# Block products for queries and keys in a trunk layer: seven for eight over two pairs and two token blocks

## The chip, the cores and the metric

The kernel runs on one core of a Trainium2 chip. The core has a matrix engine (PE, with its weight loads shown apart as PEld), a vector engine (DVE), a scalar engine (ACT), a general engine (POOL), and a queue engine (SP) that here issues almost all transfers between DRAM and the core's SBUF. Each engine takes its instructions strictly in order and waits for semaphores of others. The metric is the device time of one execution in microseconds, lower is better. The profile is one execution, taken by the hardware profiler.

## The reference, cut to what matters

One layer, sequence 2048, model width 1024, float32:

```python
h = rms_norm(x, g_attn[l]) * (1.0 + scale_a) + shift_a
proj = h @ w_in[l]
q_f, k_f, v_f, q_s, k_s, v_s, f_logit = jnp.split(proj, offsets, axis=-1)
o_fox = forgetting_attention(split_heads(q_f, N_HEADS_FOX), split_heads(k_f, N_HEADS_FOX), ...)
o_sb = stick_breaking_attention(split_heads(q_s, N_HEADS_SB), split_heads(k_s, N_HEADS_SB), ...)
x = x + gate_a * (mix @ w_out[l])
h = rms_norm(x, g_mlp[l]) * (1.0 + scale_m) + shift_m
u = causal_depthwise_conv(h @ w_up[l], conv_w[l], conv_b[l])
x = x + gate_m * ((jax.nn.silu(u_gate) * u_val) @ w_down[l])
```

Each kind of attention (stick-breaking, "sb", and forgetting, "fox") has 8 heads of 64, taken as 4 pairs of 128 columns. Both are causal.

## The kernel before

**Stages.** First h = the normalized and modulated x, made for four blocks of 512 tokens (TB) and stored to DRAM as `hs`. Then attention, in 32 units, first sb and then fox: `units` lists kind, pair p and block tb, written here (sb, p, tb). Then the output projection, the gated MLP and the last norm, which the change leaves alone; they begin at about 1462 us in the profile.

**A product in three matmuls.** Every float32 operand is kept as two parts (`split`: ACT rounds the high part, POOL or DVE subtracts it for the low part), and a product is three matmuls: high x high, high x low, low x high. `accumulate` (L340 to L342) does that for queries and keys: eight slices of the inner dimension, three matmuls of 512 columns each, 24 for a query or key block of one pair.

**Projection as a filler.** `proj` (L462) makes queries, keys and, for even p, the values of two pairs, of one unit: it loads the eight h tiles of the block (L468, tile `hp`, ten buffers, 512 KB each), accumulates the queries, then the keys (`finish_proj`, L342), and for even p the values (L413, 256 columns each). Results go to DRAM (`qk_...`, L380 and L394; `vs_...`, L440), and `load_unit` reads them back as Q, K, V (L362 to L364). Weights are loaded once a pair (`load_w`, L314 to L321, tile `raw_qk` or `raw_v`, three buffers) and stay split in SBUF.

**Attention.** For a unit, `logits` (L596, L597) makes the logits of 128 queries against up to 512 keys. In sb (`sb_head`) ACT takes two sigmoids (L630, L631), POOL masks the diagonal (L633), and DVE runs a scan along the keys (L636). `weighted` transposes (L606), copies on ACT (L610), subtracts on DVE (L611), and multiplies with V (L615). `head_var` squares on POOL (L711), and the output goes to DRAM (L740, `os`). fox has a reduction on DVE (L675) and an exponential on ACT (L679).

**What sets the order.** `project` is a generator that goes through the units in order, one `yield` for every few matmuls; `pace` says how many of its steps are due after each step of the attention, so that a unit is projected by 80% of the unit ahead of it, and otherwise evenly from unit 3 to unit 30. `interleave` mixes them with fillers of their own pace (`late_mod` from unit 12 on). A scheduler then orders the instructions of each engine, so that program order alone does not tell where an instruction stands; the order is fixed when the program is built.

## Time and profile before

| | |
|---|---|
| runs | 2942.75, 2951.94 and 2953.25 us, median 2951.94 |
| profiled execution | span 2941.4 us from the first to the last instruction; it is not known which of the runs it resembles, and the lowest run lies 1.35 us above this span |
| DMA over the span | 601.89 MB, mean 205 GB/s |
| granted PE clock | 0.993 of full speed |
| queries and keys, all blocks (L342) | 1512 matmuls of 512 columns into `ps_pj` |
| values (L413) | 1536 matmuls |

An engine's busy time is the union of its instructions; a matmul's own duration contains its way through the array, so the cost of one in a row is best read from windows in which PE does nothing else. Windows give, for a stretch of time, each engine's busy us with the number of instructions in brackets, then the granted clock, the DMA engines' busy share and GB/s. A group's row is: line, engine, operation, out<-in, shapes, xcount | busy us, mean ns of one | idle time before them and what ended it.

### The profile page before, as it was taken

To read this page: it belongs to the slowest core of one execution; us is meant where nothing else is said; L and a number is where in the kernel's file an instruction comes from. 1 tells how busy PE (TensorE), PEld (TensorE's weight loads), DVE (VectorE), ACT (ScalarE), POOL (GpSimd) and SP (SyncE) were. 2 spreads that over 40 slices of the span, in tenths; PEclk is the share of its full clock that TensorE was granted. 3 is DMA by queue.
4 is the path that set the end of the run, shared out by engine and by line. 5 is a ranking of instruction groups with operands and counts; after the bars stand their busy time and mean duration, and the time that the engine had idled before them with its cause. 6 is when DMAs were issued, how large, how long until landed. Compare 5 with 4: busy or idle time off the path is not lost.

```text
span 2941.4 us, 45922 instructions
## 1 busy us (share of the span) xinstructions
PE 2867.8 (97%) x15772; PEld 2459.7 (84%) x15772; DVE 2179.5 (74%) x3464; ACT 1686.0 (57%) x3187; POOL 901.1 (31%) x967
## 2 busy tenths in 40 slices
PE   8999999999999999999999999999999999999998
PEld 7888888888988988888888788888788888888887
DVE  5787778877886656658843788888998888575476
ACT  5776767677776656658744554444444445433342
POOL 0431322243032423231213344444254543142200
PEclk8999999999999999999999999999999999999999
DMA  9749756867469794794537775554754444975644
GB/s 293 255 139 321 236 188 207 301 211 229 162 212 356 269 277 139 232 323 140 182 120 233 245 232 128 130 136 129 236 132 125 130 130 132 309 257 185 216 158 151
DMA packets 348346, 601.89 MB, mean 205 GB/s; under 512 B 34672, under 2 KB 178800, under 8 KB 348112
## 3 DMA queue, kind: packets, MB, share of 16 engines
q1 hardware_dynamic: 324208, 558.06, 57.7%
q0 software_dynamic: 10880, 20.97, 4.3%
q10 hardware_dynamic: 13024, 19.93, 1.9%
q8 instruction: 124, 2.03, 0.3%
q14 instruction: 110, 0.90, 0.1%
HBM read 420.77 MB, written 177.02 MB: 203 GB/s over the span
## 4 chain that ended last, share of the span: by engine, by line
PE 46%; DMA 3%; DVE 2%; SPq 1%; ACT 1%; issue 1%; POOL 0%; DVEq 0%; ACTq 0%; POOLq 0%
PE ps_o L1315 19%; PE ps_t L1315 7%; PE ps_o L1614 6%; PE ps_t L1614 3%; PE ps_bc L1614 3%; PE ps_o L912 1%; PE ps_pv L615 1%; DMA r<-rstd 1%; PE ps_bc L912 1%; PE ps_pt L606 1%; PE ps_o L1609 1%; DMA wo<-wos 1%; DMA hm<-hf_m 1%; SPq L895 1%; DVE op L46 1%
## 5 line engine op out<-in xcount | busy, mean ns | idle before, releaser
L1315 PE MATMUL ps_o<-op,wu 128*128 128x512 f32 x2592 | 608.0, 389 | 2.0 <-DVE snap L1366 1.5
L1315 PEld LDWEIGHTS ps_o<-op,wu 128*128 128x128 f32 x2592 | 486.2, 188 | 103.9 <-DVE snap L1366 1.9
L611 DVE TENSOR_TENSOR at<-ps_pt,at 128x512 fp32r<-128x512 f32 (+1 forms) x576 | 366.1, 652 | 100.2 <-ACT at L610 97.3
L636 DVE TENSOR_TENSOR_SCAN a<-r,a 128x512 f32<-128x512 f32 (+2 forms) x320 | 368.3, 1167 | 77.8 <-ACT a L631 39.9
L342 PE MATMUL ps_pj<-hp,w_qk 128*128 128x512 f32 x1512 | 411.2, 403 | 14.5 <-DMA hp<-hs 12.9
L610 ACT ACTIVATE at<-ps_pt 128x512 fp32r<-128x512 f32 (+1 forms) x576 | 318.5, 576 | 139.1 <-PE ps_pt L606 123.1
L615 PE MATMUL ps_pv<-at,V 128*128 128x256 f32 x2216 | 386.8, 292 | 9.3 <-DVE at L611 4.2
L615 PEld LDWEIGHTS ps_pv<-at,V 128*128 128x128 f32 x2216 | 320.9, 190 | 39.8 <-DVE at L611 11.4
L342 PEld LDWEIGHTS ps_pj<-hp,w_qk 128*128 128x128 f32 x1512 | 275.4, 190 | 71.0 <-DMA hp<-hs 16.2
L45 ACT ACTIVATE wu<-wuraw 128x512 fp32r<-128x512 f32 x204 | 128.9, 632 | 248.5 <-PE ps_o L1315 190.1
L596 PE MATMUL ps_qk<-K,Q 128*128 128x512 f32 (+2 forms) x640 | 265.7, 416 | 5.6 <-ACT a L631 3.3
L413 PE MATMUL ps_pj<-w_v,hp 128*128 128x256 f32 (+1 forms) x1536 | 236.6, 288 | 2.1 <-DVE hp L422 1.6
L597 PE MATMUL ps_qk<-K,Q 128*128 128x512 f32 (+2 forms) x640 | 235.7, 369 | 0.0
L1315 PE MATMUL ps_t<-op,wu 128*128 128x512 f32 x888 | 220.8, 390 | 1.0 <-DVE op L46 1.0
L413 PEld LDWEIGHTS ps_pj<-w_v,hp 128*128 128x128 f32 x1536 | 209.0, 189 | 10.9 <-DVE q L373 1.5
L630 ACT ACTIVATE r<-ps_qk 128x512 f32<-128x512 f32 (+2 forms) x320 | 173.1, 541 | 58.2 <-PE ps_qk L597 55.5
L46 DVE TENSOR_TENSOR wu<-wuraw,wu 128x512 fp32r<-128x512 f32 x204 | 189.6, 930 | 18.1 <-ACT wu L45 16.7
L1315 PEld LDWEIGHTS ps_t<-op,wu 128*128 128x128 f32 x888 | 166.4, 188 | 36.5 <-DVE op L46 1.8
L606 PE MATMUL ps_pt<-edge,a 128*128 128x128 f32 x1088 | 185.1, 274 | 8.4 <-DVE a L636 7.8
L1614 PE MATMUL ps_o<-op 128*128 128x512 f32 x840 | 191.5, 389 | 0.0
L1614 PEld LDWEIGHTS ps_o<-op 128*128 128x128 f32 x840 | 157.7, 188 | 32.7
L679 ACT ACTIVATE p<-p,mn 128x128 f32<-128x128 f32 (+15 forms) x128 | 153.9, 1203 | 53.3 <-DVE mn L675 52.2
(342 smaller groups left out, 5237.6 us busy)
## 6 DMA issues: line engine op xcount, KB each, us to landing
hp<-hs SPq DMA_DIRECT2D x224, 512.0 KB
wuraw<-in_w_up_dram SPq DMA_DIRECT2D x80, 512.0 KB
ra<-g SPq DMA_DIRECT2D x136, 256.0 KB
rb<-in_w_down_dram SPq DMA_DIRECT2D x108, 256.0 KB
g<-u SPq DMA_DIRECT2D x80, 256.0 KB
hs<-hp SPq DMA_DIRECT2D x32, 512.0 KB
hp<-in_w_ada_dram SPq DMA_DIRECT2D x32, 512.0 KB
qk_fox<-q SPq DMA_DIRECT2D x32, 512.0 KB
```

The source lines that it names most:

```text
L46: (lo_engine or nc.gpsimd).tensor_sub(lo, src, f(hi))
L342: nc.tensor.matmul(acc, w[kt][:, a, n], h[:, bb], start=kt == 0 and i == 0, stop=kt == KT - 1 and i == 2)
L413: nc.tensor.matmul(av[:, t * width:(t + 1) * width], hts[kt][:, a, tok], w[1][kt][:, bb, 0:width], start=kt == 0 and m == 0, stop=kt == KT ...
L596: nc.tensor.matmul(b[:, :cw], Q[:, hl, 0, qcols], K[:, hl, :cw], start=True, stop=False)
L597: marks.append(nc.tensor.matmul(b[:, :cw], Q[:, hl, 1, qcols], K[:, hl, :cw], start=False, stop=True).ins)
L606: nc.tensor.transpose(b[:, i * P:(i + 1) * P], blk(kts[kk], qi), ident)
L610: copies = [nc.scalar.activation(at[:, 0, lo:], b[:, lo:], AF.Copy).ins, nc.vector.tensor_sub(at[:, 1, lo:], b[:, lo:], f(at[:, 0, lo:])).ins]
L611: nc.vector.tensor_sub(at[:, 1, lo:], b[:, lo:], f(at[:, 0, lo:])).ins]
L615: m = nc.tensor.matmul(o[:, 0:2 * P], V[kt // 4][:, kt % 4, hl, :], rhs, start=first and kk == 0 and w == 0, stop=last and kk == 1 and w == 1)
L636: nc.vector.tensor_tensor_scan(rev, r[:, 0:need][:, ::-1], rev, 0.0 if right[qi] is None else right[qi][:, 0:1], ALU.mult, ALU.add)
L1315: nc.tensor.matmul(b, w[:, p, j], o[:, q], start=first and i == 0, stop=last and i == 2, skip_group_check=True)
L1614: nc.tensor.matmul(b, a[:, p, t * P:(t + 1) * P], w[:, q], start=first and i == 0, stop=last and i == 2, skip_group_check=True)
```

## The change

Six of the eight pairs, (sb, 2) and (sb, 3), (fox, 0) and (fox, 1), (fox, 2) and (fox, 3), are projected in groups: two pairs and two token blocks at a time. Of one pair, queries and keys are the two column blocks of the weights; the two token blocks are the two columns on the other side; the inner dimension is cut in two halves. So a group's queries and keys are, for each pair, a 2 x 2 by 2 x 2 block product, done as seven products of four slices (12 matmuls of 512 columns) in place of eight. For one group that is 2 x 7 x 12 = 168 matmuls in place of 192; with six groups, 144 fewer. Values stay as they are.

The seven products need sums of the blocks of h (four of seven, `hsum`) and of the weights (four of seven, `wsum`). `make_sums` makes them ahead: POOL adds, POOL and ACT split the sums of h, and SP stores all of them in DRAM, as a filler of six steps a unit from unit 3 on. `need` runs whatever is missing when a group begins: both halves of the sums of h, and the sums of its own two pairs. `group` reads operands back: for each product four `hp` tiles, and a weight operand `w_op` for each pair, which is loaded and split for each product anew (two raw buffers in place of three; ACT and POOL split). Values' weights are loaded and split for every token block anew (`w_val`), where before they were loaded once a pair. The results are put together on DVE with three tiles a pair (`tmp`); queries of the first block come first, keys of both blocks last (products 4 and 6). `pace` counts a group's steps, and all four units of a group are ready when it ends.

Loads of h are as many as before (224 of 512 KB). Added are 32 loads and 32 stores of 512 KB for the sums of h, 24 loads and 24 stores of 256 KB for those of the weights; weight loads are 84 of 256 KB and 96 of 128 KB in place of 72 of 128 KB for these pairs. POOL has 252 instructions more, ACT some 150, DVE 36.

```diff
+    GROUPS = (("sb", 2), ("fox", 0), ("fox", 2))
...
-                raw = sl_.tile([P, 2, P], F32, name=f"raw_{tag}", tag="wraw", bufs=3)
+                raw = sl_.tile([P, 2, P], F32, name=f"raw_{tag}", tag="wraw", bufs=2)
...
+    def sums_tile():
+        return px.tile([P, 2, TB], F32R, name="sums", tag="xt", bufs=4)
+
+    def h_sums(t2):
+        for j in range(KT // 2):
+            t = []
+            for half in range(2):
+                for e in range(2):
+                    h = sums_tile()
+                    nc.sync.dma_start(f(h), hs[2 * t2 + e][j + half * KT // 2])
+                    nc.gpsimd.tensor_add(f(h)[:, 0], f(h)[:, 0], f(h)[:, 1])
+                    t.append(h)
+                yield
+            b11, b12, b21, b22 = (f(h) for h in t)
+            nc.gpsimd.tensor_sub(b11[:, 1], b22[:, 0], b12[:, 0])
+            nc.gpsimd.tensor_sub(b12[:, 1], b12[:, 0], b11[:, 0])
+            nc.gpsimd.tensor_sub(b21[:, 1], b22[:, 0], b12[:, 1])
+            nc.gpsimd.tensor_sub(b22[:, 1], b21[:, 0], b21[:, 1])
+            yield
+            for i, h in zip((4, 3, 1, 6), t):
+                split(h[:, 0], h[:, 1], f(h)[:, 1])
+                nc.sync.dma_start(hsum[t2][i][j], f(h))
+            yield
...
+    def w_sums(kind, p):
+        a, b = f(sums_tile()), f(sums_tile())
+        for k, t in enumerate((a, b)):
+            for half in range(2):
+                w_block(t[:, half], kind, p, k, half)
+        yield
+        nc.gpsimd.tensor_add(b[:, 1], b[:, 0], b[:, 1])
+        nc.gpsimd.tensor_sub(b[:, 0], a[:, 0], b[:, 0])
+        nc.gpsimd.tensor_sub(a[:, 0], b[:, 1], a[:, 0])
+        nc.gpsimd.tensor_sub(a[:, 1], a[:, 1], a[:, 0])
+        for i, src in ((1, a[:, 0]), (3, b[:, 1]), (4, b[:, 0]), (5, a[:, 1])):
+            nc.sync.dma_start(wsum[kind, p][i], src)
+        yield
...
+    def need(*items):
+        while not made.issuperset(items):
+            next(sums_ahead)
...
+    def w_op_(kind, p, i):
+        raw = sl_.tile([P, TB], F32, name="raw_op", tag="wraw", bufs=2)
+        if i in wsum[kind, p]:
+            nc.sync.dma_start(raw, wsum[kind, p][i])
+        else:
+            w_block(raw, kind, p, i // 6, min(i, 1))
+        w = [sl_.tile([P, TB], F32R, name="w_op", tag="w_v", bufs=8) for _ in range(2)]
+        split(w[0], w[1], raw)
+        return w
...
+    def group(kind, p, t2):
+        ps, (t0, t1) = (p, p + 1), (2 * t2, 2 * t2 + 1)
+        need(0, 1, (kind, p), (kind, p + 1))
...
+        def run(b, w, hts, first):
+            for j in range(KT // 2):
+                for n, (a, bb) in enumerate(((0, 0), (0, 1), (1, 0))):
+                    nc.tensor.matmul(b, w[a][:, j * P:(j + 1) * P], hts[j][:, bb], start=first and j == 0 and n == 0,
+                                     stop=j == KT // 2 - 1 and n == 2, skip_group_check=True)
+                if j % 2:
+                    yield
...
+            elif i == 4:
+                add(e, b, W, W)
+                keep_part(e, t1, 1, tmp[e][W])
+            else:
+                add(e, b, T, T)
+                keep_part(e, t0, 1, tmp[e][T])
+
+        top, low = slice(0, KT // 2), slice(KT // 2, KT)
+        for chain in ((0, 2), (1, 3, 5), (4, 6)):
+            banks = [pj(), pj()]
+            for i in chain:
+                h = load(hsum[t2][i] if i in hsum[t2] else hs[t0][top] if i == 0 else hs[t0 if i == 2 else t1][low])
+                for e, q in enumerate(ps):
+                    yield from run(banks[e], w_op(kind, q, i), h, i == chain[0])
+                    done(e, i, banks[e])
+                if i == 0:
+                    h0 = h
+            if chain[0] == 0:
+                yield from group_values(kind, p, t0, h0 + h)
+            elif chain[0] == 1:
+                yield from group_values(kind, p, t1, load(hs[t1][top]) + h)
...
-        due = sum(proj_steps(u) for u in units[:i + 2])
+        due = max(upto[u] for u in units[:i + 2])
...
-        interleave(attend(kind, p, tb, results[kind, p], Fbs), n, [(lm if i >= LATE else None, PER, False), (tail, 17 + IDLE if nxt is None else 13, True)], follow)
+        interleave(attend(kind, p, tb, results[kind, p], Fbs), n, [(lm if i >= LATE else None, PER, False), (sums_ahead if i >= 3 else None, 6, False), (tail, 17 + IDLE if nxt is None else 13, True)], follow)
```

In the changed program the new matmuls stand at L630 (products, tile `w_op`) and L592 (values, tile `w_val`); logits move to L804 and L805, the weighted sum's multiplication to L823, transposes to L814, the output store to L948, `load_unit` to L370 to L372.

How the instructions move, at three places. First PE at the border between units (sb, 1, 3) and (sb, 2, 0), before. `K_5265` and `Q_5264` are those of (sb, 2, 0), `Q_4562` of the unit before:

```order
L596 MATMUL ps_qk_6129<-K_3158,Q_4562 128x512
L597 MATMUL ps_qk_6129<-K_3158,Q_4562 128x512
L342 MATMUL ps_pj_6517<-hp_6344,w_qk_4263 128x512 x3
L342 MATMUL ps_pj_6517<-hp_6349,w_qk_4268 128x512 x3
L615 MATMUL ps_pv_5930<-at_6044,V_4035 128x256 x4
L615 MATMUL ps_pv_5930<-at_6084,V_3812 128x256 x4
L596 MATMUL ps_qk_6205<-K_5265,Q_5264 128x256
L597 MATMUL ps_qk_6205<-K_5265,Q_5264 128x256
L615 MATMUL ps_pv_5930<-at_6110,V_3812 128x256
L606 MATMUL ps_pt_6149<-edge_249,a_6125 128x128 x2
```

The same border in the changed program (the first L804 here is the first logits of (sb, 2, 0)):

```order
L814 MATMUL ps_pt<-edge,a 128x128 x4
L823 MATMUL ps_pv<-at,V 128x256 x11
L630 MATMUL ps_pj<-hp,w_op 128x512 x72
L592 MATMUL ps_pj<-w_val,hp 128x256 x96
L630 MATMUL ps_pj<-hp,w_op 128x512 x96
L592 MATMUL ps_pj<-w_val,hp 128x256 x13
L804 MATMUL ps_qk<-K,Q 128x256
L805 MATMUL ps_qk<-K,Q 128x256
L804 MATMUL ps_qk<-K,Q 128x256
L805 MATMUL ps_qk<-K,Q 128x256
```

Six projection matmuls at a time stood among two units' attention; now 277 stand in one piece, and the next unit's first logits stand behind them.

Second, SP at the same border in the changed program: from the output store of (sb, 1, 3), `os5_3`, onward (`sums` are tiles of sums, `wsum` their places in DRAM, `raw_op` a weight operand):

```order
L948 DMA os5_3_115<-oT_5471 128x512
L509 DMA sums_4791<-in_w_in_dram 128x4x128 x2
L509 DMA sums_4792<-in_w_in_dram 128x4x128 x2
L523 DMA wsum_sb2_3_271<-sums_4778 128x512
L523 DMA wsum_sb2_4_272<-sums_4778 128x512
L523 DMA wsum_sb2_1_270<-sums_4777 128x512
L509 DMA sums_4805<-in_w_in_dram 128x4x128
L523 DMA wsum_sb3_3_275<-sums_4792 128x512
L509 DMA sums_4805<-in_w_in_dram 128x4x128
L523 DMA wsum_sb2_5_273<-sums_4777 128x512
L563 DMA raw_op_5588<-wsum_sb2_1_270 128x512
```

and further down, 118 DMAs and 39.2 MB from that store, the keys of (sb, 2, 0), `K_6639`:

```order
L642 DMA qk_sb3_1_4814<-q2_6360 128x1024
L577 DMA raw_val_6968<-in_w_in_dram 128x256
L577 DMA raw_val_6973<-in_w_in_dram 128x256
L642 DMA qk_sb2_0_4811<-q2_6441 128x1024
L642 DMA qk_sb3_0_4813<-q2_6602 128x1024
L577 DMA raw_val_6978<-in_w_in_dram 128x256
L371 DMA K_6639<-qk_sb2_0_4811 64x512 x4
L371 DMA K_6671<-qk_sb2_1_4812 64x512 x4
```

Sums of weights and the whole rest of the group stand between a unit's output and the next unit's keys; before, the keys of (sb, 2, 0), (sb, 2, 1) and (sb, 2, 2) were loaded ahead of that store.

Third, PE at the beginning of unit (sb, 2, 2), before (`w_qk` is the weight tile of the projection):

```order
L596 MATMUL ps_qk_6911<-K_6451,Q_6450 128x256
L597 MATMUL ps_qk_6911<-K_6451,Q_6450 128x256
L342 MATMUL ps_pj_7253<-hp_7146,w_qk_7061 128x512 x3
L342 MATMUL ps_pj_7253<-hp_7151,w_qk_7066 128x512 x3
L342 MATMUL ps_pj_7253<-hp_7172,w_qk_7071 128x512 x3
L342 MATMUL ps_pj_7253<-hp_7177,w_qk_7076 128x512 x3
L606 MATMUL ps_pt_6840<-edge_249,a_6836 128x128 x2
L606 MATMUL ps_pt_6866<-edge_249,a_6836 128x128 x2
L596 MATMUL ps_qk_6944<-K_6224,Q_6450 128x512
L597 MATMUL ps_qk_6944<-K_6224,Q_6450 128x512
```

and in the changed program:

```order
L592 MATMUL ps_pj<-w_val,hp 128x256 x72
L630 MATMUL ps_pj<-hp,w_op 128x512 x54
L804 MATMUL ps_qk<-K,Q 128x256
L805 MATMUL ps_qk<-K,Q 128x256
L804 MATMUL ps_qk<-K,Q 128x256
L805 MATMUL ps_qk<-K,Q 128x256
L804 MATMUL ps_qk<-K,Q 128x512
L805 MATMUL ps_qk<-K,Q 128x512
L804 MATMUL ps_qk<-K,Q 128x512
L805 MATMUL ps_qk<-K,Q 128x512
L814 MATMUL ps_pt<-edge,a 128x128 x3
```

The projection stands in one piece ahead of the unit and no longer inside it: from here to the end of (sb, 2, 3) the changed program has 18 projection matmuls of 512 columns, before it had 210, with 34 of 256 columns.

More of the change, by code (lines that the diff above doesn't have):

```diff
@@ new lines, with make_sums, in_row @@
+    made = set()
+    def make_sums():
+        for t2 in range(NTB // 2):
+            yield from h_sums(t2)
+            made.add(t2)
+        for kind, p in GROUPS:
+            for e in range(2):
+                yield from w_sums(kind, p + e)
+                made.add((kind, p + e))
+    sums_ahead = make_sums()
+    def need(*items):
+        while not made.issuperset(items):
+            next(sums_ahead)
+    row = {}
+    @contextmanager
+    def in_row():
+        with ExitStack() as order:
+            for ins in row.values():
+                order.enter_context(tc.issue_after(ins))
+            n = len(nc.cur_bb.bb.instructions)
+            yield
+        for ins in nc.cur_bb.bb.instructions[n:]:
+            if ins.engine in (nc.sync.engine, nc.scalar.engine):
+                row[ins.engine] = ins
@@ L809, with jobs_of @@
     results = {}
+    for kind_ in ("sb", "fox"):
+        for p_ in range(4):
+            results[kind_, p_] = []
+    class Group(tuple):
+        pass
+    def jobs_of():
+        out = []
+        for u in units:
+            kind, p, tb = u
+            if not any(kind == k and p in (q, q + 1) for k, q in GROUPS):
+                out.append((u, [u]))
+            elif p % 2 == 0 and tb % 2 == 0:
+                out.append((Group((kind, p, tb // 2)), [(kind, q, t) for q in (p, p + 1) for t in (tb, tb + 1)]))
+        return out
+    work = jobs_of()
     def proj_gen(u):
         kind, p, tb = u
+        if isinstance(u, Group):
+            return group(*u)
         if tb == 0:
             weights[kind, p] = load_w(kind, p)
-            results[kind, p] = []
         if (kind, p) == ("sb", 0):
```

112 lines of the change are left out of this document (104 added, 8 removed).

## The prediction

> **What bounds the kernel now.** I read the page's busy times first, then windows cut where a unit of attention begins, then the groups and the queue's waits.
>
> ```profile
> span 2941.4 us, 45922 instructions
> PE 2867.8 (97%) x15772; PEld 2459.7 (84%) x15772; DVE 2179.5 (74%) x3464; ACT 1686.0 (57%) x3187; POOL 901.1 (31%) x967
> ```
>
> PE is busy nearly all the time, so 144 matmuls fewer look like a sure gain. The windows say under what condition. A unit is one kind, pair and block of 512 tokens; the borders are the starts of the units' first logits (L596), found by counting its 640 records.
>
> ```profile
> core 0: us, PE busy (x) PEld busy (x) DVE busy (x) ACT busy (x) POOL busy (x), PEclk, DMA share, GB/s
> 220.10:305.40 85.30, 84.09 (x491) 72.19 (x490) 67.93 (x86) 60.88 (x121) 15.05 (x16) 1.00 0.88 308
> 305.40:488.40 183.00, 180.79 (x1236) 164.34 (x1236) 144.36 (x192) 131.86 (x290) 43.77 (x61) 1.00 0.61 205
> 488.40:540.60 52.20, 50.91 (x354) 46.18 (x354) 42.20 (x56) 37.71 (x91) 21.93 (x32) 1.00 0.80 253
> 540.60:674.90 134.30, 128.70 (x784) 110.80 (x782) 108.59 (x134) 101.40 (x218) 47.78 (x51) 1.00 0.75 254
> 865.80:1032.10 166.30, 163.58 (x1042) 145.15 (x1041) 114.06 (x283) 107.56 (x210) 60.37 (x78) 1.00 0.90 313
> 1320.50:1362.70 42.20, 41.73 (x289) 37.19 (x288) 37.62 (x98) 31.76 (x52) 6.97 (x11) 1.00 0.24 83
> 1378.70:1399.30 20.60, 20.21 (x139) 17.00 (x139) 19.04 (x56) 19.01 (x41) 5.67 (x13) 1.00 0.44 134
> 2600.00:2700.00 100.00, 100.00 (x443) 82.84 (x442) 64.15 (x85) 38.04 (x73) 34.08 (x24) 1.00 0.65 219
> ```
>
> The reader is to see two things. In the stick-breaking stage (rows one to four) DVE is busy 79 to 81% of the time and ACT over 70%, while PE is full: attention alone would leave PE idle, and projections fill it. Where projections have run out (1320.5 and 1378.7) DVE is busy 89 and 92%, and DVE or ACT sets the pace. So a projection matmul is free of charge while it lies between attention work and costs its full time where it stands alone. The gain hangs on where the scheduler put the projections, not on their number.
>
> ```profile
> 487.40 1.12 PE L615 MATMUL ps_pv<-at,V 128*128 128x256 f32 x8
> 488.35 0.28 PE L596 MATMUL ps_qk<-K,Q 128*128 128x256 f32 x1
> ```
>
> At 488.35, where unit (sb, 2, 0) begins, the unit before it is still at its weighted sums: before, units overlap.
>
> **The change, part by part.** A 512-column matmul costs 100.00 / 443 = 0.226 us back to back (2600:2700); a 256-column one I take at half, 0.12. Then 144 fewer are worth **-33 us** if every one shows. The rows of PE's order say otherwise. After the last weighted sum of unit (sb, 1, 3) the changed program has 168 matmuls of 512 columns and 109 of 256 in one piece, before the first logits of (sb, 2, 0): the group hands on its keys last (products 4 and 6), so attention waits for a whole group. That piece alone is 168 x 0.226 + 109 x 0.12 = 51 us in which DVE and ACT have next to nothing to do. Later pieces are 54 and 72 matmuls before (sb, 2, 2) (21 us), and 25 and 19 us in the FoX stage. I go by stretches, each against its row.
>
> *Stretch A, 220.1 to 488.4, 268 us.* Its projections shrink from 366 + 288 matmuls (512 and 256 columns) to 240 + 96, since the rest now stands behind it: 126 x 0.226 + 192 x 0.12 = 51 us less for PE. Then DVE decides: 67.9 + 144.4 = 212 us, less 6 for copies that move away. POOL gets the sums of h and the weights here, and these rows show what a DVE instruction with two SBUF inputs pays beside POOL:
>
> ```profile
> L46 DVE TENSOR_TENSOR wu<-wuraw,wu 128x512 fp32r<-128x512 f32 x204 | 189.6, 930 | 18.1 <-ACT wu L45 16.7
> L46 DVE TENSOR_TENSOR wu<-ws,wu 128x512 fp32r<-128x512 f32 x80 | 55.7, 696 | 4.2 <-ACT wu L45 4.2
> L636 DVE TENSOR_TENSOR_SCAN a<-r,a 128x512 f32<-128x512 f32 (+2 forms) x320 | 368.3, 1167 | 77.8 <-ACT a L631 39.9 <-POOL a L633 33.9
> ```
>
> The first stands among POOL's weight sums, 930 ns against 696, a third more. A has 112 of the 320 scans (131 us); with POOL busy half of the time that is nothing to 22 us, and I take 15. So DVE needs 221 us, and at 0.9 busy (the rows without projections) A takes 246: **-22 us**.
>
> *Stretch B, the piece between (sb, 1, 3) and (sb, 2, 0).* Two bounds beside PE's 51 us. First DMA. SP issues in order, and waits in order:
>
> ```profile
> SPq L457 <- DMA vd<-xt: 25.6, 4, 9.1
> SPq L468 <- PE ps_pj L342: 22.4, 11, 10.1
> ```
>
> (from 305.4 to 674.9; us in total, times, longest), so nothing behind the store of (sb, 1, 3)'s output starts before that unit is done. From that store to the load of (sb, 2, 0)'s keys stand 118 DMAs, 39.2 MB by their shapes: sums of weights 11.5, operands of h 12.6, weights 5.4, the rest stores and reloads. What the queue can carry:
>
> ```profile
> 220.00:230.00 10.00, 9.44 (x56) 8.02 (x56) 8.08 (x10) 6.60 (x17) 6.30 (x5) 1.00 1.02 408
> 550.00:560.00 10.00, 9.86 (x64) 8.49 (x64) 8.58 (x13) 7.69 (x18) 2.19 (x3) 1.00 1.03 415
> 860.00:910.00 50.00, 46.62 (x293) 40.01 (x293) 39.23 (x99) 36.47 (x81) 15.03 (x24) 1.00 1.04 364
> ```
>
> 39.2 MB take 95 us at 415 GB/s, 108 at 364, 125 at the 313 of the row 865.8. By the Trainium skill, page "DMA: Bandwidth & Descriptors", section Specifications, HBM gives one core about 358 GB/s, an estimate of 109 us for this piece; the 10 us rows of this trace lie above that figure, the 50 us row beside it.
>
> Second POOL, in order as well:
>
> ```profile
> L783 POOL TENSOR_TENSOR hp<-hp 128x512 f32<-128x512 f32 x56 | 74.9, 1356 | 55.6 <-ACT hp L782 52.7 <-issue 2.8
> L46 POOL TENSOR_TENSOR w_qk<-raw_qk,w_qk 128x256 fp32r<-128x256 f32 x56 | 49.9, 904 | 58.7 <-ACT w_qk L45 52.9 <-PE ps_qk L597 5.7
> L458 POOL TENSOR_TENSOR xt<-xt 128x1024 f32<-128x1024 f32 x4 | 10.2, 2538 | 43.2 <-DMA xt<-vd 43.2
> ```
>
> Between the two units it has 24 sums of weights, 14 splits of operands and 8 other splits of 512 columns (46 x 1.36), 13 of 256 (x 0.90) and two of 1024 (x 2.54): 79 us. So B takes 79 us at least, 95 to 125 by DMA, and more if waits line up. I take **112 us**, near the 50 us row.
>
> *Stretch C, units (sb, 2, 0) and (sb, 2, 1).* 24 and 11 matmuls more between the attention's: **+7 us**. *Stretch D, the second piece, before (sb, 2, 2).* PE 21 us; from the output store of (sb, 2, 1) to the key load stand 20.7 MB (with four loads of FoX sums and six of w_ada that come due there): 50 us at 415, 57 at 364, 66 at 313. I take **55 us**. *Stretch E, (sb, 2, 2) and (sb, 2, 3).* Here 210 + 34 projection matmuls stood, now 18: no filler is left. DVE's 108.6 less 7 for copies, at 0.9, is 113 us against 134.3: **-21 us**.
>
> *Stretch F, from (sb, 3, 0) on.* Over (fox, 0), 865.8 to 1032.1, SP's rows hold 67.5 MB instead of 52.4 (313 GB/s x 166 us says the same of before). At 364 GB/s that is 185 us (+19), at 313 216 (+49); the nearer is the busiest row's, I take +22. Elsewhere PE has 29 us less; (fox, 1) then comes near DVE, and I take -18. **+4 us.** Behind 1462 us nothing changes: 0.
>
> ACT's part (some 150 instructions more, 0.4 to 0.6 us each, spread over 1100 us in which it is busy two thirds) and the 60 adds on DVE (24 splits go to POOL; 36 x 0.69 = 25 us, most of it in the pieces where DVE is idle) I cost at nothing more; were that cover gone, they would add up to 25 us on DVE in A and E.
>
> ```profile
> L1371 DVE TENSOR_TENSOR y<-ps_o,snap 128x512 f32<-128x512 f32 x40 | 27.7, 691 | 58.4 <-PE ps_o L1315 58.4
> ```
>
> **Sum:** -22 + 112 + 7 + 55 - 21 + 4 = +135 on the span of 2941.4, 3076. The median of the runs shown, 2951.9, lies 10.5 above the span; on that scale **3087 us**, 4.6% slower.
>
> **The rivals.**
> - *The saved matmuls show (the other side).* The DMAs of B and D land while PE works through the pieces (51 and 21 us), and DVE keeps up fully in A and E: A falls by PE's whole 51 (no scan slowed by POOL), E to DVE's 102 (-32), F to PE's -12. Sum -51 + 51 + 7 + 21 - 32 - 12 = -16: 2936. For it: PE is the bound on the page. Against: SP's order, and no row in which DVE and ACT run full together. It decides from where B and D together stay under 88 us. Chance 0.07.
> - *The pieces run at PE's speed, DVE at 0.9.* B 51, D 21, F -12: -22 + 51 + 7 + 21 - 21 - 12 = +24, 2976. Both this and the first need 39.2 MB in 51 us, 770 GB/s, where 415 is the best row, unless SP issues earlier than its order lets it. 0.08; with DVE between 0.9 and 1 it ends within 0.5%: 0.06.
> - *Waits line up on SP.* There are two buffers for raw weights, and 27 such loads stand in B: two in flight, 2.9 MB for each pair (39.2 / 13.5), 9.3 us at 313 GB/s, 125 us in all, and some 10 for the sums stored and reloaded ahead of the first: B 135, D in proportion 66: +34 on the forecast, 3121. 0.15.
> - *POOL and DVE shut each other out.* If each POOL sum in A delays a scan for its whole length: 60 added instructions of 1.36 us meet DVE half of the time, +40 us on DVE, A at 290 instead of 246, 3131. The rows bear out a third of an instruction, not the whole. 0.06. The Trainium skill's page "SBUF — State Buffer", section "SBUF: two separate sides", speaks for this one: the port pair that DVE (with two SBUF inputs) and GpSimd share is an exclusive lock, held for a whole instruction.
>
> **How the numbers follow.** The forecast has the remaining 0.58; its own bounds are B 95 to 125, D 50 to 66, A and E each 12 either way, F -10 to +35, some 3030 to 3150. The range 2955 to 3180 takes in the rivals with waits and the one at PE's speed; left out are the first rival, "no change" and a tail above. A measurement of this kernel tells about 0.5% from no change: faster 0.07, same 0.06, slower 0.87.
>
> **What would show it.** B: between the last weighted sum of (sb, 1, 3) and the first logits of (sb, 2, 0), some 110 us with DVE under 20% busy, DMA near full, PE waiting for `hp` and `w_op`. D: the same, some 55 us. E: DVE near 90%, PE at about 60%. A: some 20 us shorter, scans longer than 1167 ns. Wrong would be: B near 51 us (then DMA ran ahead, and the prediction is some 90 us too high), or a FoX stage far off +4.

## The result, and the profile after

The changed kernel takes 3224.96 us (median of four runs, 3223.09 to 3233.22), before 2947.35 beside it: a ratio of 1.095, 95% interval 1.0924 to 1.0976. It is slower, as forecast, but by 278 us and not by 135; the time lies above the range.

The page's first lines, of the kernel after:

```profile
span 3221.3 us, 46692 instructions
PE 2923.7 (91%) x15628; PEld 2472.0 (77%) x15628; DVE 2248.7 (70%) x3500; ACT 1765.4 (55%) x3340; POOL 1257.3 (39%) x1219
```

With 144 matmuls fewer, PE is busy 56 us *longer*, and idle 297.6 us (span less busy time) where it was idle 73.6. Both hang together, as the windows show. Cut at the same borders as in the prediction (starts of units, the last weighted sum of (sb, 1, 3) at 507.7, the first matmul after it at 546.9), columns as before:

```profile
core 0: us, PE busy (x) PEld busy (x) DVE busy (x) ACT busy (x) POOL busy (x), PEclk, DMA share, GB/s
155.20:229.80 74.60, 64.87 (x411) 56.84 (x410) 61.12 (x72) 55.40 (x119) 61.03 (x49) 0.93 0.72 238
229.80:507.70 277.90, 234.42 (x1426) 199.81 (x1424) 242.56 (x270) 201.03 (x426) 171.75 (x138) 0.96 0.72 253
507.70:546.90 39.20, 0.04 (x1) 0.00 (x0) 1.22 (x3) 2.90 (x5) 27.46 (x23) 0.53 0.94 301
546.90:644.80 97.90, 67.05 (x277) 52.88 (x278) 11.55 (x17) 19.73 (x37) 44.98 (x40) 0.78 0.88 302
644.80:713.40 68.60, 61.86 (x398) 54.13 (x396) 48.42 (x65) 42.37 (x101) 30.87 (x36) 0.99 0.78 265
713.40:757.60 44.20, 30.21 (x126) 23.75 (x126) 4.57 (x7) 8.27 (x16) 18.03 (x17) 0.75 0.83 293
757.60:785.80 28.20, 0.00 (x1) 0.03 (x1) 0.00 (x0) 7.99 (x13) 21.18 (x18) 0.50 0.84 312
785.80:881.50 95.70, 85.48 (x527) 68.77 (x527) 92.17 (x115) 84.84 (x183) 18.35 (x25) 0.98 0.21 60
1068.30:1294.50 226.20, 197.78 (x1186) 170.64 (x1185) 129.15 (x305) 129.49 (x251) 103.95 (x113) 0.93 0.87 293
1500.20:1595.30 95.10, 63.55 (x364) 53.56 (x363) 33.34 (x85) 46.68 (x85) 48.25 (x48) 0.82 0.63 207
```

The reader is to see the two pieces that the order of PE foretold: 277 matmuls in 97.9 us with DVE 12% busy, behind 39 us in which PE does nothing at all; then 126 matmuls in 44.2 us, with 28 us of nothing behind them. From 785.8 on there is almost nothing but attention: DVE is busy 96% of the time and sets the pace. The last two rows are (fox, 0), which took 166.3 us before, and (fox, 2, 2), which took 61.1. In the stretches without matmuls the clock column falls to 0.50.

The stretches of the prediction against what came:

| stretch | forecast | measured |
|---|---|---|
| ahead of A (to the start of (sb, 0, 3)) | 0 | +9.7 |
| A, (sb, 0, 3) to the end of (sb, 1, 3) | -22 | +9.6 (277.9 against 268.3) |
| B, the first piece | +112 | +137.1 (39.2 + 97.9) |
| C, (sb, 2, 0), (sb, 2, 1) | +7 | +16.4 |
| D, the second piece | +55 | +72.4 (44.2 + 28.2) |
| E, (sb, 2, 2), (sb, 2, 3) | -21 | -38.6 |
| F, (sb, 3, 0) to the end of fox | +4 | +70 |
| behind | 0 | +3.3 |
| sum | +135 | +280 |

What PE waited for, from 440 to 1740 us (us in total, times, longest):

```profile
PE ps_pj L630 <- ACT w_op L45: 40.2, 7, 8.8
PE ps_pj L630 <- DVE xt L598: 39.2, 1, 39.2
PE ps_qk L804 <- DMA K<-qk_sb: 28.2, 1, 28.2
PE ps_pj L592 <- ACT w_val L45: 26.2, 13, 7.6
PE ps_pt L814 <- DVE a L844: 23.4, 29, 2.7
PE ps_qk L804 <- DMA K<-qk_fox: 18.6, 2, 18.1
```

The second row is the 39 us of nothing: a matmul waits for DVE to copy the values into `xt`, and that copy in its turn waits for a buffer that the FoX weight sums hold (the trace puts 37.5 us of DVE's idle time ahead of it down to `wsum_fox<-sums`). It looks like a cause with a name; e3 takes that wait away and gains nothing. When the sums ran, by the instructions on tile `sums`:

```profile
L492 SPq DMA_DIRECT2D sums<-hs x32: 319/324/722, 180.3 to 485.8; - x32
L46 POOL TENSOR_TENSOR sums<-sums x32: 1273/1314/4113, 199.7 to 504.9; 128x512 fp32r<-128x512 f32 x32
L518 POOL TENSOR_TENSOR sums<-sums x6: 1261/1262/1263, 513.3 to 562.0; 128x512 f32<-128x512 f32 x6
```

(minimum, median and maximum ns, then first and last start.) The last sum of h is split at 504.9 us, the weights' come after it: a group that `need` makes wait for all of them cannot run its products 1, 3, 5, 4, 6 beside the attention that ends at 507.7.

### The profile page after: what moved, and what is told of

Same layout as the page of the kernel before. It is cut to its first block, busy times and chain, and to the rows that moved or that the text cites. A ratio compares the mean times of both kernels' runs of the same rounds, so it can differ in the third digit from the quotient of the medians.

```text
span 3221.3 us, 46692 instructions
## 1 busy us (share of the span) xinstructions
PE 2923.7 (91%) x15628; PEld 2472.0 (77%) x15628; DVE 2248.7 (70%) x3500; ACT 1765.4 (55%) x3340; POOL 1257.3 (39%) x1219
## 5 line engine op out<-in xcount | busy, mean ns | idle before, releaser
L844 DVE TENSOR_TENSOR_SCAN a<-r,a 128x512 f32<-128x512 f32 (+2 forms) x320 | 417.7, 1323 | 103.3 <-POOL a L841 76.4
L823 PE MATMUL ps_pv<-at,V 128*128 128x256 f32 x2216 | 402.0, 296 | 21.7 <-DVE at L819 16.2
L823 PEld LDWEIGHTS ps_pv<-at,V 128*128 128x128 f32 x2216 | 328.3, 192 | 61.9 <-DVE at L819 32.6
L630 PE MATMUL ps_pj<-hp,w_op 128*128 128x512 f32 x1008 | 282.4, 420 | 97.1 <-ACT w_op L45 40.2
L804 PE MATMUL ps_qk<-K,Q 128*128 128x512 f32 (+2 forms) x640 | 271.6, 425 | 58.4 <-DMA K<-qk_sb 28.2
L630 PEld LDWEIGHTS ps_pj<-hp,w_op 128*128 128x128 f32 x1008 | 192.2, 200 | 147.9 <-ACT w_op L45 43.9
L805 PE MATMUL ps_qk<-K,Q 128*128 128x512 f32 (+2 forms) x640 | 238.4, 374 | 0.0
L814 PE MATMUL ps_pt<-edge,a 128*128 128x128 f32 x1088 | 190.7, 283 | 51.3 <-DVE a L844 45.0
L592 PE MATMUL ps_pj<-w_val,hp 128*128 128x256 f32 x1152 | 192.9, 306 | 34.5 <-ACT w_val L45 26.2
L592 PEld LDWEIGHTS ps_pj<-w_val,hp 128*128 128x128 f32 x1152 | 168.0, 206 | 47.1 <-ACT w_val L45 29.9
L814 PEld LDWEIGHTS ps_pt<-edge,a 128*128 128x128 f32 x1088 | 130.8, 143 | 86.7 <-DVE a L844 46.3
```

The source lines that it names most:

```text
L592: nc.tensor.matmul(av[:, t * 2 * P:(t + 1) * 2 * P], hts[kt][:, a, tok], ws[kt][:, bb], start=kt == 0 and m == 0, stop=kt == KT - 1 and m ...
L630: nc.tensor.matmul(b, w[a][:, j * P:(j + 1) * P], hts[j][:, bb], start=first and j == 0 and n == 0, stop=j == KT // 2 - 1 and n == 2, skip ...
L804: nc.tensor.matmul(b[:, :cw], Q[:, hl, 0, qcols], K[:, hl, :cw], start=True, stop=False)
L805: marks.append(nc.tensor.matmul(b[:, :cw], Q[:, hl, 1, qcols], K[:, hl, :cw], start=False, stop=True).ins)
L814: nc.tensor.transpose(b[:, i * P:(i + 1) * P], blk(kts[kk], qi), ident)
L823: m = nc.tensor.matmul(o[:, 0:2 * P], V[kt // 4][:, kt % 4, hl, :], rhs, start=first and kk == 0 and w == 0, stop=last and kk == 1 and w == 1)
```

## The experiments

Each run is compared with runs of the kernel before on the same chip. One hundredth of the ratio is 29.5 us. Rows of the table come from different chips, so compare their ratios and not their times. In the code, `...` marks lines left out.

| run | median us | ratio, 95% interval |
|---|---|---|
| the change | 3225.0 | 1.0950 (1.0924 to 1.0976) |
| e1_fox_groups | 3110.8 | 1.0558 (1.0527 to 1.0588) |
| e2_plain_groups | 3084.0 | 1.0467 (1.0433 to 1.0501) |
| e3_own_values | 3241.8 | 1.1002 (1.0961 to 1.1044) |
| e4_sums_alone | 3041.1 | 1.0298 (1.0268 to 1.0327) |
| e5_defer_wsums | 3235.7 | 1.0982 (1.0950 to 1.1014) |
| e7_needed_sums | 3212.7 | 1.0879 (1.0847 to 1.0910) |
| e8_plain_early | 3057.7 | 1.0354 (1.0321 to 1.0387) |
| e9_needed_early | 3139.3 | 1.0647 (1.0608 to 1.0687) |
| e10_free_sums | 3093.1 | 1.0474 (1.0443 to 1.0504) |
| e11_sums_dma | 2981.7 | 1.0113 (1.0082 to 1.0143) |
| e12_sums_pool | 3001.3 | 1.0179 (1.0138 to 1.0220) |
| e13_plain_high | 3064.2 | 1.0393 (1.0355 to 1.0430) |
| e14_plain_blocks | 3036.9 | 1.0303 (1.0278 to 1.0328) |
| e15_blocks_once | 3009.0 | 1.0208 (1.0183 to 1.0233) |
| e16_long_rows | 3227.7 | 1.0944 (1.0918 to 1.0971) |
| e17_early_high | 3041.0 | 1.0317 (1.0292 to 1.0342) |
| e18_three_raw | 3191.8 | 1.0808 (1.0760 to 1.0856) |
| e19_blocks_three_raw | 3005.8 | 1.0178 (1.0141 to 1.0216) |

Where the time went in the most telling of them, in us between starts of units (from each trace):

| | to (sb, 0, 3) | A + B | (sb, 2, 0-1) + D | (sb, 2, 2-3) | (sb, 3) | (fox, 0) | (fox, 1, 0) to (fox, 2, 1) | (fox, 2, 2) |
|---|---|---|---|---|---|---|---|---|
| before | 220 | 268 | 52 | 134 | 191 | 166 | 227 | 61 |
| the change | 230 | 415 | 141 | 96 | 187 | 226 | 206 | 95 |
| e10, sums not made | 225 | 279 | 145 | 96 | 188 | 228 | 208 | 96 |
| e2, eight products | 224 | 283 | 120 | 111 | 193 | 220 | 226 | 85 |
| e8, e2 due sooner | 223 | 355 | 54 | 111 | 223 | 165 | 257 | 43 |
| e9, both cures | 232 | 358 | 159 | 96 | 223 | 155 | 241 | 51 |
| e4, sums alone | 224 | 311 | 63 | 143 | 193 | 180 | 233 | 60 |

### Groups or sums?

```diff
-    GROUPS = (("sb", 2), ("fox", 0), ("fox", 2))
+    GROUPS = (("fox", 0), ("fox", 2))
```

> Only the four FoX pairs are grouped; (sb, 2) and (sb, 3) are projected as before, and the sums of h and of the FoX weights are still made from unit 3 on. Theory (the two pieces ahead of (sb, 2, 0) and (sb, 2, 2) cost most, and the FoX stage loses 70 us by itself): the stick-breaking stage comes back to some 10 to 30 us over before (the sums alone), the FoX stage stays 70 us longer, in all 3030 to 3045 us. Rival (the FoX stage's loss was handed down from the late stick-breaking groups): 2960 to 2980 us. Rival (the sums, not the groups, are what costs): no nearer to before than 3100 us.

It took 3110.8 us, which is the second rival's number. Against the theory, the start of (sb, 3, 0) still comes 65 us late instead of 10 to 30, and what follows loses 102 instead of 70. The sums were still made here, and taking the first groups away moves work to other places; this run alone separates little.

```diff
-        for chain in ((0, 2), (1, 3, 5), (4, 6)):
+        for k, t in ((0, 0), (0, 1), (1, 0), (1, 1)):
...
+                    yield from run(banks[e], w_op(kind, q, k, half), h, half == 0)
```

> Same groups, same order (queries of both blocks first, keys last, weights loaded and split anew for each product), but eight plain products in place of seven and no sums of h or weights; 144 matmuls more than the change, and the low parts of the keys are subtracted on DVE instead of POOL. Theory (the group as a unit that hands on its keys last makes the long piece ahead of (sb, 2, 0)): the piece stays, the 39 us wait for the values' buffers goes, in all 3160 to 3190 us. Rival (the sums, made too late, push the group behind the attention; grouping alone does not): no piece ahead of (sb, 2, 0), the ones ahead of (sb, 2, 2) and in the FoX stage stay, in all 3040 to 3090 us. Rival (sums are the whole cost): within 1% of before, at most 2977 us.

It took 3084.0 us, as the first rival has it: there is no piece ahead of (sb, 2, 0) (A + B 283 us), while the one ahead of (sb, 2, 2) stays, shorter, and (fox, 0) and (fox, 2, 2) stay long. Keys are handed on last here too, so that alone does not make the first piece. The run also says what the groups cost with no sums at all: 4.7 hundredths, half of the loss.

```diff
-        need(0, 1, (kind, p), (kind, p + 1))
...
-                h = load(hsum[t2][i] if i in hsum[t2] else hs[t0][top] if i == 0 else hs[t0 if i == 2 else t1][low])
+                h = load(hs[t0 if i in (0, 1, 2) else t1][top if i in (0, 3, 4) else low])
```

> The change with its seven products and additions, but no sums are made: products that would read a sum of h or of weights read blocks of h and weights in its place (as many loads of the same sizes). Beside the run with eight plain products it has 144 matmuls fewer and 60 additions on DVE more. Theory (the sums' making, not their use, costs the 140 us between the change and the plain groups): no piece ahead of (sb, 2, 0), 3050 to 3085 us, and so at most some 30 us for 144 matmuls. Rival (the additions on DVE and the keys' late completion make the piece): 3150 to 3200 us.

It took 3093.1 us, a little above the theory's range. Its row in the table is nearly the change's row everywhere but in the first two columns: the first piece and A's slowness come from the making of the sums (with the wait for them in `need`), 128 us between the two spans, and what comes later is the groups. Beside e2 it has the 144 matmuls fewer, with 36 more instructions on DVE, and the two ratios cannot be told apart: 1.0474 and 1.0467, each known to about 9 us either way. The first lines of the pages of e2 and of e10:

```profile
span 3085.9 us, 46594 instructions
PE 2919.4 (95%) x15772; PEld 2483.3 (80%) x15772; DVE 2198.1 (71%) x3464; ACT 1745.4 (57%) x3307; POOL 1058.9 (34%) x1087
```

```profile
span 3093.1 us, 46289 instructions
PE 2898.1 (94%) x15628; PEld 2463.0 (80%) x15628; DVE 2211.3 (71%) x3500; ACT 1746.4 (56%) x3307; POOL 1061.9 (34%) x1099
```

PE is busy 21 us less and idle 28.5 us more (195.0 against 166.5): what seven products save comes back as waiting.

### What the sums cost

The kernel before, with the functions of the sums from the change:

```diff
-        t = wide() if p == 0 else px.tile([P, D], F32, name="xt", tag="xt", bufs=4)
+        t = wide() if p in (0, 2) else px.tile([P, D], F32, name="xt", tag="xt", bufs=4)
...
+(sums_ahead if i >= 3 else None, 6, False)
```

> The kernel before, with all its projections unchanged, and the sums of h and of the weights made and stored as in the change, though nothing reads them; the values of (sb, 2) take their tile from the buffers of h, so that the sums have theirs alone. Theory (the sums cost by themselves, through POOL's queue, the vector engine beside it and the transfers): 3000 to 3015 us, the +65 us that the run with FoX groups alone showed ahead of (sb, 3, 0). Rival (the sums cost nothing where nobody waits for them): at most 2965 us.

It took 3041.1 us, some 87 more than before and above the theory's range. The next two runs take its two halves apart. In e11 the tiles go in and out and nothing is added; in e12 POOL and ACT work on tiles that are never loaded or stored:

```diff
-                    nc.gpsimd.tensor_add(f(h)[:, 0], f(h)[:, 0], f(h)[:, 1])
...
-                split(h[:, 0], h[:, 1], f(h)[:, 1])
```

> As the run with sums alone (3041 us, 87 over before), but only their transfers: the tiles are loaded and stored, nothing is added or split, so no work on POOL or ACT. If the transfers cost the 87 us: 3025 to 3045 us. If POOL's additions cost them (beside DVE's scans and ahead of POOL's own masks): 2955 to 2980 us. If both in part: between.

```diff
-                    nc.sync.dma_start(f(h), hs[2 * t2 + e][j + half * KT // 2])
-                    nc.gpsimd.tensor_add(f(h)[:, 0], f(h)[:, 0], f(h)[:, 1])
+                    nc.gpsimd.tensor_add(f(h)[:, 0], flat, flat)
...
-                nc.sync.dma_start(hsum[t2][i][j], f(h))
```

> As the run with sums alone, but only the 120 additions on POOL with the 32 splits on ACT and POOL, on tiles without transfers; nothing is loaded or stored for them. If POOL's additions cost the 87 us: 3020 to 3045 us, scans near 1450 ns in the stretch from 220 to 500 us. If the transfers cost them: 2955 to 2980 us, though scans are longer.

They took 2981.7 and 3001.3 us: 33 and 53 us over before, which add up to the 87 within what the runs can tell. The scans from 220 to 500 us, in before, the change, e11 and e12 (busy us, mean ns of one; then DVE's idle time ahead of them):

```profile
L636 DVE TENSOR_TENSOR_SCAN a<-r,a 128x512 f32<-128x512 f32 (+1 forms) x118 | 133.5, 1146 | 37.2 <-ACT a L631 21.1 <-POOL a L633 14.7
```

```profile
L844 DVE TENSOR_TENSOR_SCAN a<-r,a 128x512 f32<-128x512 f32 (+3 forms) x117 | 170.7, 1480 | 25.8 <-POOL a L841 17.6 <-ACT a L839 6.9
```

```profile
L689 DVE TENSOR_TENSOR_SCAN a<-r,a 128x512 f32<-128x512 f32 (+3 forms) x117 | 136.5, 1185 | 17.2 <-POOL a L686 9.6 <-ACT a L684 6.2
```

```profile
L691 DVE TENSOR_TENSOR_SCAN a<-r,a 128x512 f32<-128x512 f32 (+3 forms) x104 | 153.9, 1504 | 26.4 <-POOL a L688 15.7 <-ACT a L686 10.1
```

Transfers almost leave the scan alone (1185 ns against 1146); POOL's additions and subtractions lengthen it by some three tenths on average (1480 and 1504). Over the whole of e12 that makes 41.6 us more of scans (409.9 against 368.3 for all 320), most of its 53:

```profile
L691 DVE TENSOR_TENSOR_SCAN a<-r,a 128x512 f32<-128x512 f32 (+2 forms) x320 | 409.9, 1302 | 84.0 <-POOL a L688 42.3 <-ACT a L686 38.6
```

The mean mixes two kinds. Of the change's 86 scans of 512 columns from 220 to 500 us, the 32 that no POOL addition or subtraction overlaps take 1.26 us, the 42 that are overlapped by over 1 us take 1.90. The timelines of DVE and of POOL in e12 look as if the two took turns (start, us; x2 is two in a row):

```profile
305.37 3.92 DVE L691 TENSOR_TENSOR_SCAN a<-r,a 128x512 f32<-128x512 f32 x2 [0.69 <-ACT a L686]
```

```profile
304.75 1.28 POOL L46 TENSOR_TENSOR sums<-sums 128x512 fp32r<-128x512 f32 x1
305.98 2.22 POOL L497 TENSOR_TENSOR sums<-sums 128x512 f32<-128x512 f32 x1
308.17 2.21 POOL L46 TENSOR_TENSOR sums<-sums 128x512 fp32r<-128x512 f32 x1
```

Two scans take 1.96 us each instead of 1.26, and the two POOL instructions beside them 2.2 instead of 1.28: both engines lose, 0.7 and 0.9 us each time.

### The wait that has a name, and when the sums are made

```diff
-        t = wide() if p == 0 else px.tile([P, D], F32, name="xt", tag="xt", bufs=4)
+        t = wide() if p in (0, 2) else px.tile([P, D], F32, name="xt", tag="xt", bufs=4)
```

> The change, but the values of (sb, 2) and (sb, 3) take their tile from the ten buffers of h instead of the four that the sums use. Theory (in the 39 us in which PE stands still, the copy of the values waits for a buffer held by the FoX weight sums): that gap goes, 3180 to 3190 us. Rival (the transfers and POOL's additions ahead of it are late anyway): the gap stays under another name, 3210 to 3230 us.

```diff
-(sums_ahead if i >= 3 else None, 6, False)
+(sums_ahead if i in (3, 4, 5) or i >= 9 else None, 6, False)
```

> The change, but the sums of the FoX weights (8.4 MB of transfers, 16 additions on POOL) are made from unit 9 on instead of beside the first group. Theory (the wait for the values' buffers and the crowded queue): the 39 us gap goes and the piece behind it shrinks a little, 3160 to 3190 us. Rival (late anyway): 3210 to 3230 us.

Neither helps (3241.8 and 3235.7 us, if anything longer). In e5, A + B is 9 us shorter and (sb, 2, 0-1) + D 9 us longer. In e3, from 440 to 800 us, the row with `xt` is gone, and PE waits longer for `w_op` (31.0 us; 19.0 in the same stretch of the change) and for `hsum`:

```profile
PE ps_pj L630 <- ACT w_op L45: 31.0, 4, 20.4
PE ps_qk L804 <- DMA K<-qk_sb: 27.6, 2, 27.4
PE ps_pj L592 <- ACT w_val L45: 20.0, 10, 5.2
PE ps_pj L630 <- DMA hp<-hsum: 19.7, 2, 10.1
```

The buffer was only the last of several late things. So the next run lets a group start on fewer sums, makes these first, and has e3's tiles for the values:

```diff
-        need(0, 1, (kind, p), (kind, p + 1))
+        need(t2, (kind, p), (kind, p + 1))
```

> The change, but a group waits only for the sums that it uses: those of its own two token blocks and two pairs, made in that order (values of (sb, 2) and (sb, 3) in the buffers of h, so that the two don't hold each other up). Theory (the sums of h, which ran from 180 to 506 us, hold the first group back until the attention ahead of it is over): the piece ahead of (sb, 2, 0) shrinks from 168 + 109 matmuls to 120 + 84, and the 39 us before it go: 3155 to 3185 us. Rival (transfers and POOL bound that stretch in any order): 3210 to 3240 us.

It took 3212.7 us, 0.7 hundredths less and within the rival's range. The sums of the first group are all on their way to DRAM by 401 us here, 127 us before the attention ahead of the piece ends at 528.1, and still 96 + 84 matmuls stand in one piece of 84 us (before (sb, 2, 0); 168 + 109 in 137 us in the change):

```profile
528.10:612.10 84.00, 45.09 (x181) 36.35 (x179) 5.95 (x9) 15.71 (x29) 52.62 (x45) 0.74 0.94 327
```

So waiting for fewer sums takes some 53 us off the first piece. Of that, (sb, 1, 3) together with the piece keeps a gain of 31 us (180.9 instead of 212.2), and (sb, 2, 1) takes 13 more: the second group is late instead. Projections that come due sooner are tried next, first without sums:

```diff
-        due = max(upto[u] for u in units[:i + 2])
+        due = max(upto[u] for u in units[:i + (4 if i >= 4 else 2)])
```

> The groups with eight plain products and no sums, projections due two units sooner from unit 4 on. Theory (a group's second half of tokens comes due within two short units, and the pieces ahead of (sb, 2, 2), (fox, 0, 2) and (fox, 2, 2) are that): the +67, +47 and +24 us there go, 2965 to 2995 us. Rival (the groups' transfers or the matrix engine bind there, whenever they are due): 3060 to 3085 us.

It took 3057.7 us, just under the rival's range. The pieces do shrink: (sb, 2, 0-1) 120 to 54, (fox, 0) 220 to 165, (fox, 2, 2) 85 to 43, 164 us in all. But 133 come back where the groups are made instead: A 283 to 355, (sb, 3) 193 to 223, (fox, 1, 0) to (fox, 2, 1) 226 to 257. When a group is due moves its cost; most of it stays.

Both cures (e7 and the last diff) in the change:

> The change with both cures together: a group waits for its own sums alone, and projections are due two units sooner from unit 4 on. Theory (late sums make the piece ahead of (sb, 2, 0), due times the ones in the FoX stage; the sums' own 90 us stay): the FoX stage comes back to within 20 us of before, the stick-breaking stage stays long: 3130 to 3170 us. Rival (the groups' work binds wherever it stands): 3200 to 3230 us.

It took 3139.3 us, in the theory's range and 3.0 hundredths under the change: the stretch from (sb, 3, 0) to the output projection takes 809 us against 787 before (22 more, where the theory had at most 20), and the stick-breaking stage stays long. It is the best version here that makes the sums and takes seven products for all six pairs, and it is still 6.5 hundredths slower than the kernel before.

### What is left in the groups

The low part of the groups' weights is left out, in e2 (run e13) and in e8 (run e17):

```diff
-        split(w[0], w[1], raw)
+        nc.scalar.activation(w[0], raw, AF.Copy)
+        w[1] = w[0]
...
-                split(w[:, 0], w[:, 1], raw)
+                nc.scalar.activation(w[:, 0], raw, AF.Copy)
```

> The groups with eight plain products and no sums (3084 us), without the low part of the groups' weights: POOL's subtraction for each weight operand is left out and the high part is used in its place, as many matmuls and transfers. If POOL's part of splitting the weights anew for every product makes the groups dear: 3030 to 3055 us. If the transfers or the due times do: 3070 to 3090 us.

> Eight plain products, no sums, due two units sooner, without the low part of the weights. If due times (-26 us) and POOL's splits (-20 us) are separate costs: 3030 to 3045 us. If they are the same waits: 3055 to 3062 us.

e13 took 3064.2 us, 0.7 hundredths under e2 and between the two theories. e17 took 3041.0, where the two costs would add up; but it lies only 0.4 hundredths under e8 and their intervals overlap, so that this second gain is not certain.

Next, groups of one token block with plain products, handed on one at a time; then the same with h loaded once for queries, keys and values:

```diff
-                out.append((Group((kind, p, tb // 2)), [(kind, q, t) for q in (p, p + 1) for t in (tb, tb + 1)]))
+                out.append((Group((kind, p, tb)), [(kind, q, tb) for q in (p, p + 1)]))
```

> Groups of two pairs and one token block, with plain products: the same weights loaded and split anew for each product and block, the same number of loads of h as before, but queries, keys and values of a block are handed on together, and the next block comes due with its own units. Theory (handing on four units at once, with their keys last, is what is left of the groups' cost): 2975 to 3005 us. Rival (weights loaded and split anew): 3045 to 3075 us.

```diff
-                h = load(hs[tb][top])
+                h = load(hs[tb][top]) if k == 0 else h2[top]
```

> As the run before it, but the tiles of h are loaded once for queries, keys and values of both pairs: 96 loads of 512 KB fewer (50 MB). By the price that the sums' transfers showed (33 us for 46 MB): some 35 us below the run before it, 2940 to 2970 us. If transfers are hidden where nothing waits for them: within 10 us of it.

e14's 3036.9 us lie between the theories: handing on two blocks at once is a third of the plain groups' cost (1.6 of 4.7 hundredths). Loading h once gives another 28 us for 50 MB, less than the 35 worked out and far from nothing: 0.6 us for each MB that the queue is spared, where e11 paid 0.7.

### The rate in the first piece

```diff
-        nc.sync.dma_start(t.rearrange("p (k n) -> p k n", n=P),
-                          w_in[half * TB:(half + 1) * TB, col:col + P].rearrange("(k p) n -> p k n", p=P))
+        nc.sync.dma_start(t, w_in[half * TB:half * TB + P, col - base_of(kind, p) + p * TB:col - base_of(kind, p) + (p + 1) * TB])
```

> The change, but blocks of weights (for the weight sums and three of the seven operands) are read from DRAM as 128 rows of 2 KB instead of 512 pieces of 512 bytes: as many bytes, other numbers. Theory (short rows hold the transfers of the piece ahead of (sb, 2, 0) at 301 GB/s, where the forecast took 364): that piece shrinks by 10 to 25 us, in all 3195 to 3215 us. Rival (the rate is set by the order of the queue and its waits): 3220 to 3230 us.

```profile
DMA packets 30718, 41.92 MB, mean 301 GB/s; under 512 B 2019, under 2 KB 21093, under 8 KB 30713
```

```profile
DMA packets 19443, 42.75 MB, mean 305 GB/s; under 512 B 2053, under 2 KB 5767, under 8 KB 19437
```

(the change from 505.6 to 645 us, and this run from 510 to 650.1). With a quarter of the short packets (under 2 KB), rate and time are the same: that theory falls.

```diff
-        raw = sl_.tile([P, TB], F32, name="raw_op", tag="wraw", bufs=2)
+        raw = sl_.tile([P, TB], F32, name="raw_op", tag="wraw", bufs=3)
...
-                o2 = sb.tile([HD, 2 * P], F32, name="o2", bufs=2)
+                o2 = sb.tile([HD, 2 * P], F32, name="o2", bufs=1)
```

> The change with three buffers for raw weights, as before it, in place of two (paid for by one instead of two small output tiles, o2, in the attention). The prediction's rival that waits line up behind two raw buffers gave the first piece 135 us and the second 66, close to what was measured (137 and 72). If two raw buffers hold the pieces: they shrink by some 20 and 10 us, the pieces in the FoX stage too, 3165 to 3195 us. If transfers and the sums' order hold them: 3215 to 3235 us.

> The groups of one token block with h loaded once (3009 us), with three raw buffers and one o2 in the same way. If two raw buffers are part of what is left of the groups' cost: 2975 to 2995 us. If not: 3003 to 3015 us.

e18 took 3191.8 us, within the first theory's range and 1.4 hundredths under the change; in the groups by blocks (e19) there is no difference that these runs can tell. In e18 the first piece is 125.5 us instead of 137.1, at 321 GB/s, and the second some 50 instead of 72; A is 7 us longer. PE's waits of e18, from 70 to 1720 us, show where the gain ends:

```profile
PE ps_qk L804 <- DMA K<-qk_sb: 39.3, 1, 39.3
PE ps_qk L804 <- DMA K<-qk_fox: 36.2, 2, 18.5
PE ps_pj L630 <- DVE xt L598: 31.2, 1, 31.2
PE ps_pt L814 <- DVE a L844: 27.0, 40, 2.4
PE ps_pj L592 <- ACT w_val L45: 13.4, 3, 5.8
```

The wait for `w_op` (40.2 us in the change, 9.0 here) has left the head of the list, and the waits for keys have grown by 29 us.

## Why the prediction was wrong in size

**Where it held.** The bound at work was read rightly: PE's 97% was no reason for a gain, pieces without attention cost their full time, and 144 matmuls gave a PE that waits nothing that these runs can tell (e10 against e2). B, D and E stand where they were put, with DVE at 12%, 10% and 96%. E's size was off the other way, and by luck hid 18 us of the rest: the prediction had 102 us of work on DVE at 90% busy, and DVE had 92 at 96%, so that E gave 39 us instead of 21.

**The rate of the queue (B, D, F).** The bytes were nearly right: 39.2 MB forecast in B and 41.9 found, 20.7 in D and 300 GB/s x 72.4 us = 21.7, 67.5 in (fox, 0) and 293 x 226 = 66.3. The step that failed is the division by 364 GB/s, the busiest 50 us of the kernel before. All three stretches ran near 300, and at that rate the prediction's own sums give 130, 69 and 230 us instead of 108, 57 and 185; measured were 137, 72 and 226. That is the largest part of the 145 us by which the forecast fell short: 25 in B, 17 in D and 38 in (fox, 0), 80 in all. The other parts are 41 in A and ahead of it, 34 in (fox, 2, 2), 9 in C and 3 behind, less 18 in E and 6 in the rest of F.

The rate in B is not low throughout; it stops and starts, as 40 slices of it show (the change, 505.6 to 645 us):

```profile
GB/s 288 375 314 229 272 258 308 312 298 286 334 312 294 208 364 354 300 397 421 404 411 198 248 122 150 5 354 396 286 400 409 388 345 407 256 226 322 273 304 200
```

Mostly fewer packets were under way, and not slower ones: by the column of DMA shares they fill 90% of the 16 engines' time in this stretch and 104% in the busiest row. By that ratio alone, as an estimate, 364 becomes 315 here, 290 in D (83%; 300 measured) and 304 in (fox, 0) (87%; 293 measured). That fits loads that wait for buffers and stores that wait for POOL; how much each of them holds up was not separated. The rival with two raw buffers (B 135, D 66) had both sizes almost exactly, and e18 shows that the buffers are part of it: a third buffer takes 12 us off the first piece and some 22 off the second, where the rival had 23 and 11. Short rows are not part of it (e16). What else holds the rate is open.

**The FoX stage (F).** Besides (fox, 0), (fox, 2, 2) lost 34 us, for which the prediction had no term: it named a piece of 19 us of PE's time there and gave it no cost of its own. In the row 1500.2 to 1595.3 DMA is busy only 63%: it is not the rate. e8 and e9 take the loss away by sooner due times, so it is a second group that comes due within two short units, with its keys late.

**POOL in A, and ahead of it.** The forecast had 15 us for slower scans, within "nothing to 22"; the scans took 37.2 us longer (170.7 against 133.5). The price was read from a mean (a third more), which is too low for a scan that does meet an addition (1.90 against 1.26, half more); POOL was busy 62% of A and not half of it; and the sums began at 180 us, a unit sooner than A. So -22 became +9.6, with +9.7 ahead of it. The rival "shut each other out" (A 290) was nearer than the forecast (246), with 278 measured. Here the Trainium skill's page "SBUF — State Buffer", section "SBUF: two separate sides", speaks of a lock held for the whole instruction, and of DMA and engines that cannot slow each other there. The traces agree with the second for the scan (1185 ns in e11, 1146 before). With the first they agree in kind: the scan and the POOL instruction in e12's timelines lose 0.7 and 0.9 us to each other, over half an instruction but not a whole one of 1.26 or 1.28.

**Why there is a first piece.** The prediction blamed the group's handing on its keys last. e2 and e10 hand them on in the same order and have no such piece, so it comes from making the sums. A part is the wait in `need`: the last sums came at 505 us and later, when the attention was over, and with own sums alone, ready by 401 us, the piece falls from 137 to 84 us (e7). Why those 84 us remain was not taken apart; DMA is busy 94% in them, and the other half's sums are still being made. For the time of this kernel the wrong reason made no difference, since the piece was read from the order of PE; for a cure it does.

**What stays open.** Groups by blocks, with h loaded once and three raw buffers, no sums and no saved matmul, are still 1.8 hundredths (some 53 us) slower than before. POOL's splits, the weights loaded anew for every product and the handing on of two pairs at once are among what still differs; a part of the first was seen in e13, the rest was not taken apart. That sums and groups together cost more than apart (9.5 against 3.0 + 4.7 hundredths) fits with sums that come too late for the groups. e9 takes back 3.0 of the 9.5, but by sooner due times too; how much of the excess is lateness alone was not measured.

## What to carry to other kernels

A product scheme that saves matmuls can pay only in stretches where PE is the last to be ready. Where projections serve as filler between attention work, a replacement that needs more transfers, more POOL work and a later hand-over can turn the filler into a stage of its own, as it did here. Price a new transfer by the rate of a stretch with as many waits as the new one, not by the busiest row, and a POOL operation beside DVE by the instructions that meet it, not by a mean. And a wait named in the profile may be only the last of several late things: take it away alone before you believe it.
